# Turning the softmax maxima into a row: a transfer in place of four TensorE transposes

## The chip, the cores and the metric

The kernel runs on one core of a Trainium2 chip. The metric is the device time of one execution in microseconds (us); the median of three runs is compared. Five engines work side by side and are tied by semaphores: TensorE (PE, with its weight loads shown apart as PEld), VectorE (DVE), ScalarE (ACT), GpSimd (POOL) and SyncE, whose queue (SP) issues every transfer of this kernel.

## The reference

Two layers over 1024 latent tokens and 256 context tokens, model width 1024. In each layer one input projection feeds a grouped-query attention (16 query heads and 4 key heads of 64, so four query heads share a key head) and a gated linear recurrence; both are gated, projected, merged and added back. What the change touches is the softmax of the attention:

```python
def gqa(q, k, v):
    s = jnp.einsum('bqkgd,bskd->bkgqs', q, k).astype(jnp.float32)
    p = jax.nn.softmax(s, axis=-1).astype(v.dtype)
    return jnp.einsum('bkgqs,bskd->bqkgd', p, v)
```

A latent query sees 1280 keys, a context query the 256 context keys; the second layer has no context queries.

## The kernel before

The activations lie with features on the partitions, and each layer runs in four stages: queries, keys and values; the recurrence; attention; the output products. The change lies in the attention stage, which runs twice, at about 600 to 1330 us and 2255 to 2905 us of the span.

**Units.** The attention is cut into units of one head and 512 latent queries (64 units: 32 in each layer) or of two heads and 256 context queries (8 units, first layer only). `Unit.load` brings a unit's queries into two tiles of 512 columns, `qa` (high and low halves of the numbers, on 128 partitions) and `qb` (the high halves again on partitions 0 to 63). Partition 64 of `qb` is a row of 512 numbers that the unit fills itself: minus the maximum of each query's scores. Its partner in the keys, row 64 of `k2`, is all ones, so that the product over 65 rows subtracts the maximum while the scores are summed.

**The first pass, for the maxima.** `s1(j, b)` multiplies a block of 128 queries (the stationary operand, a slice of `qa`) with up to 512 keys (the moving operand) into a PSUM tile `s1ps`, queries on the partitions; 0.3 us later in the plan VectorE reduces it to one column of `mp` (line 980). A long unit has twelve such pieces: four blocks by 512, 512 and 256 keys. `smax` reduces `mp` to `mz`, 128 partitions by 4 blocks (line 985). `aug` turns that into the row: four TensorE transposes (line 149) write 1x128 pieces of a PSUM tile `mtps`, and ScalarE copies its 512 numbers, negated, to row 64 of `qb` (line 991).

**The second pass.** `s2(kt)` multiplies 128 keys with all 512 queries in two products, the one with `qa` and the one with `qb` and its row 64; ScalarE takes the exponential twice (`pf` in full precision, `ph` rounded), VectorE the difference `pl` (line 1004), GpSimd adds the `pf` up, and `av(kt)` multiplies both with the values. A long unit has ten of these.

**The order.** TensorE executes in the order in which the program emits; for the other engines and the SP queue the compiler's scheduler may place instructions otherwise. The emission follows a plan: `Timeline` holds a clock that each TensorE instruction advances by a model cost (`mm`, and 0.109 us for each transpose in `tr`), and a heap of events. A unit begins at `g0`, in plan units; long units are 10 apart. Its load stands at `g0` - 14.5, its first-pass pieces from -12.4 to -4.3, `smax` at -3.2, `aug` at -2.0, its `s2(kt)` at `g0` + kt. So units overlap: while one unit runs its second pass, the next runs its first. Between the events TensorE is filled with the input products of the gates (`gps`). `pace` turns plan units into clock time from the sum of all model costs; by the trace a plan unit lasts some 1.95 us in the second layer.

**Tiles.** `ptile("s")` hands out six PSUM banks in turn to `s1ps`, `s2ps`, `mtps`, `lps` and `gps`. `qa` and `qb` have three buffers each.

Of the kernel before, what the change touches and what calls it, by code (L numbers as in the profile page):

```python
# [26 lines left out]
F32 = mybir.dt.float32  # L27
F32R = mybir.dt.float32r
AF = mybir.ActivationFunctionType
OP = mybir.AluOpType  # L30
AX = mybir.AxisListType
# [27 lines left out]
def r32(ap):  # L59
    return ap.bitcast(F32)  # L60
# [40 lines left out]
def trunk_kernel(ctx: ExitStack, tc: tile.TileContext, xT, cc, par, wmod, win, wgate, wo,  # L101
                 rope_c, rope_s, out):
    nc = tc.nc
    V, S, G, DMA = nc.vector, nc.scalar, nc.gpsimd, nc.sync
    ctx.enter_context(tc.manual_schedule(engines={mybir.EngineType.PE}))
    tl = Timeline()
# [8 lines left out]
    def ptile(tag, name):  # L115
        tag = "s" if tag == "g" else tag
        bufs = {"s": 6, "av": 2}[tag]
        return psum.tile([128, 512], F32, name=name, tag=tag, bufs=bufs)
# [16 lines left out]
    def mm(o, a, b, start, stop, cost=None):  # L135
        n = 1
        for d in b.shape[1:]:
            n *= d
        if cost is not None:
            tl.now += cost  # L140
        elif b.dtype == F32R:
            tl.now += 0.216 * n / 512
        else:
            tl.now += max(0.2, 0.858 * n / 512)
        nc.tensor.matmul(o, a, b, start=start, stop=stop)  # L145

    def tr(o, a):
        tl.now += 0.109
        nc.tensor.transpose(o, a, ident)  # L149
# [302 lines left out]
    class Group:  # L452


        def __init__(self, l, tiles, g, chs, store, name):
            self.l, self.tiles, self.g, self.chs, self.store = l, tiles, g, chs, store
            self.qg, self.work = {}, None
            self.parts, self.sq = [chs], {}
            self.o0 = 0 if "C" in chs else CTX
            self.n = TOK - self.o0  # L460
            self.rows = [dtile(l, f"{name}{t}", [2, 2, self.n]) for t in tiles]
# [247 lines left out]
    for l in range(DEPTH):  # L709
# [206 lines left out]
        with tc.tile_pool(name="att", bufs=2, reuse_waits="tile") as work:  # L916
            kv = {}

            def load_kv(g):
                k1 = work.tile([128, TOK], F32R, name="k1", tag="k1")  # L920
                k2 = work.tile([128, TOK], F32R, name="k2", tag="k2")
                t, r0 = g // 2, (g % 2) * 64
                DMA.dma_start(r32(k1[0:64]), dd["k"][t][0, r0:r0 + 64])
                DMA.dma_start(r32(k1[64:128]), dd["k"][t][0, r0:r0 + 64])
                DMA.dma_start(r32(k2[0:64]), dd["k"][t][1, r0:r0 + 64])
                G.memset(r32(k2[64:65]), 1.0)
                v = work.tile([128, 10, 128], F32R, name="vv", tag="vv")
                DMA.dma_start(r32(v), dd["v"][g])
                kv[g] = k1, k2, v
# [4 lines left out]
            def add(g, fn):  # L934
                cnt[0] += 1
                ev.append((g, cnt[0], fn))
# [3 lines left out]
            class Unit:  # L940


                def __init__(self, i, t, c, e, g0):
                    self.i, self.t, self.c, self.e, self.g0 = i, t, c, e, g0
                    self.nkt = 2 if e == 2 else 10
                    self.P = {}
                    late = not last and t and c == "L0" or e == 2
                    add(-24 if i == 0 else g0 - 11.8 if late else g0 - 14.5, self.load)
                    nb = 1 if e == 2 else 3
                    pieces = [(j, b) for j in range(4) for b in range(nb)]  # L950
                    for x, (j, b) in enumerate(pieces):
                        add(g0 - (9.6 - 6.2 * x / len(pieces) if late else 12.4 - 8.8 * x / len(pieces)), lambda j=j, b=b: self.s1(j, b))
                    add(g0 - 3.2, self.smax)
                    add(g0 - 2.0, self.aug)
                    for kt in range(self.nkt):
                        add(g0 + kt, lambda kt=kt: self.s2(kt))
                        add(g0 + kt + 2.8, lambda kt=kt: self.av(kt))
                    add(g0 + self.nkt + 1.85, self.evac)
                    add(g0 + self.nkt + (5.0 if e == 2 else 3.6), self.lsum)
                    self.groups = ((0,), (1,)) if e == 2 else ((0, 1, 2), (3, 4, 5), (6, 7), (8, 9))  # L960
                    self.accs = {}
# [13 lines left out]
                def s1(self, j, b):  # L975
                    k1 = kv[self.t // 2][0]
                    n = 256 if self.e == 2 or b == 2 else 512
                    ps = ptile("s", "s1ps")
                    mm(ps[:, :n], self.qa[:, j * 128:(j + 1) * 128], k1[:, b * 512:b * 512 + n], True, True)
                    tl.at(0.3, lambda: V.reduce_max(self.mp[:, j, b:b + 1], ps[:, :n], axis=AX.X))  # L980

                def smax(self):
                    nb = 1 if self.e == 2 else 3
                    self.mz = work.tile([128, 4], F32, name="mz", tag="mz", bufs=3)
                    V.reduce_max(self.mz, self.mp[:, :, :nb], axis=AX.X)

                def aug(self):
                    pt = ptile("s", "mtps")
                    for j in range(4):
                        tr(pt[0:1, j * 128:(j + 1) * 128], self.mz[:, j:j + 1])  # L990
                    S.activation(self.qb[64:65], pt[0:1, :], AF.Copy, scale=-1.0)

                def s2(self, kt):
                    k1, k2, _ = kv[self.t // 2]
# [103 lines left out]
            g0, cost, i = 5.0, 0.0, 0  # L1098
            for t in range(8):
                if t % 2 == 0:  # L1100
                    add(g0 - 19 if t else -25, lambda t=t: load_kv(t // 2))
                for c, e in [("L0", 0), ("L0", 1), ("L1", 0), ("L1", 1)] + ([] if last else [("C", 2)]):
                    Unit(i, t, c, e, g0)
                    i += 1
                    ctxu = e == 2
                    g0 += 2 if ctxu else 10
                    cost += (4 * 0.108 + 2 * 0.864 + 1.34 if ctxu else 4 * 0.54 + 10 * 0.864 + 1.34)
            ev.sort(key=lambda x: (x[0], x[1]))
            first_g = ev[0][0]
            span = ev[-1][0] - first_g  # L1110
# [226 lines left out]
```

## Time and profile before

| | |
|---|---|
| median of three runs | 3194.48 us (3193.29 to 3196.1) |
| the profiled execution | 3197.96 us, of which the span is 3196.2 us |
| PE busy | 3059.7 us, 96% of the span |
| DVE, ACT, POOL busy | 2457.1, 1749.6, 1020.0 us |
| mean granted TensorE clock | 0.986 |

The span runs from the first to the last instruction of the profiled execution. An engine's busy time is an average over stages with different limits. "Idle before" an instruction is put down to what ended it. The ends of matmuls are modelled, so the distance between two starts says more than a duration.

### The profile page before, as it was taken

To read this page: it belongs to the slowest core of one execution; us is meant where nothing else is said; L and a number is where in the kernel's file an instruction comes from. 1 tells how busy PE (TensorE), PEld (TensorE's weight loads), DVE (VectorE), ACT (ScalarE), POOL (GpSimd) and SP (SyncE) were. 2 spreads that over 40 slices of the span, in tenths; PEclk is the share of its full clock that TensorE was granted. 3 is DMA by queue.
4 is the path that set the end of the run, shared out by engine and by line. 5 is a ranking of instruction groups with operands and counts; after the bars stand their busy time and mean duration, and the time that the engine had idled before them with its cause. 6 is when DMAs were issued, how large, how long until landed. Compare 5 with 4: busy or idle time off the path is not lost. (4 is left out here: it accounts for less than half of the span.)

```text
span 3196.2 us, 42921 instructions
## 1 busy us (share of the span) xinstructions
PE 3059.7 (96%) x14880; PEld 2430.8 (76%) x14880; DVE 2457.1 (77%) x3675; ACT 1749.6 (55%) x3060; POOL 1020.0 (32%) x777
## 2 busy tenths in 40 slices
PE   7999999999999999999899999899999999999999
PEld 3788788777777777787778778777777777777887
DVE  7665887589898988556685785997799999996544
ACT  4323667466666666545555324676477766673222
POOL 0211444234434333234432121433244444441000
PEclk9999999999999999999999999999999999999999
DMA  5443111311222122264555452111412121115554
GB/s 196 144 152 121 50 50 62 115 59 59 73 64 78 60 64 64 87 195 153 172 191 168 147 166 87 60 47 53 121 56 75 58 75 58 52 59 170 181 177 138
DMA packets 233049, 331.95 MB, mean 104 GB/s; under 512 B 53296, under 2 KB 99184, under 8 KB 232576
## 3 DMA queue, kind: packets, MB, share of 16 engines
q1 hardware_dynamic: 232832, 329.21, 32.0%
q8 instruction: 117, 1.92, 0.2%
q14 instruction: 100, 0.82, 0.1%
HBM read 252.54 MB, written 76.58 MB: 103 GB/s over the span
## 5 line engine op out<-in xcount | busy, mean ns | idle before, releaser
L145 PE MATMUL gps<-h,whi 128*128 128x512 f32 x3328 | 1041.4, 394 | 21.1 <-DVE g L876 15.3
L145 PEld LDWEIGHTS gps<-h,whi 128*128 128x128 f32 x3328 | 612.1, 190 | 148.4 <-issue 10.7
L1004 DVE TENSOR_TENSOR pl<-pf,ph 128x512 fp32r<-128x512 f32 x656 | 630.2, 961 | 83.1 <-ACT ph L1003 79.5
L145 PE MATMUL gps<-h,wlo 128*128 128x512 f32 x1664 | 654.5, 393 | 1.3 <-DVE wlo L227 1.3
L1002 ACT ACTIVATE pf<-s2ps 128x512 f32<-128x512 f32 x656 | 392.8, 599 | 348.1 <-issue 157.0
L1018 POOL TENSOR_TENSOR acc<-pf 128x512 f32<-128x512 f32 x256 | 352.0, 1375 | 713.1 <-ACT pf L1002 711.5
L980 DVE TENSOR_REDUCE mp<-s1ps 128x1 f32<-128x512 f32 (+1 forms) x800 | 454.1, 583 | 63.7 <-PE s1ps L145 60.8
L1003 ACT ACTIVATE ph<-s2ps 128x512 fp32r<-128x512 f32 x656 | 390.0, 595 | 0.0
L227 DVE TENSOR_TENSOR wlo<-wraw,whi 128x512 fp32r<-128x512 f32 x392 | 335.3, 878 | 61.4 <-ACT whi L226 32.7
L226 ACT ACTIVATE whi<-wraw 128x512 fp32r<-128x512 f32 x324 | 193.6, 627 | 333.8 <-PE gps L145 258.1
L145 PEld LDWEIGHTS gps<-h,wlo 128*128 128x128 f32 x1664 | 314.3, 189 | 69.9 <-DVE wlo L227 2.0
L145 PE MATMUL s1ps<-k,qa 128*128 128x512 f32 (+1 forms) x800 | 284.9, 363 | 12.3 <-DMA qa<-q0L 10.3
L145 PE MATMUL avps<-ph,vv 128*128 128x512 f32 x656 | 266.9, 407 | 0.0
L145 PE MATMUL avps<-pl,vv 128*128 128x512 f32 x656 | 260.2, 397 | 5.0 <-DVE pl L1004 4.9
L145 PE MATMUL s2ps<-qa,k 128*128 128x512 f32 x656 | 261.1, 398 | 1.8 <-DVE mp L980 1.6
L145 PE MATMUL s2ps<-qb,k 65*128 65x512 f32 x656 | 260.3, 397 | 0.0
L145 PE MATMUL gps<-e,whi 128*128 128x512 f32 x768 | 243.9, 399 | 0.2 <-DVE e L227 0.2
L360 POOL TENSOR_TENSOR macc<-macc,wmt 128x512 f32<-128x512 f32 x112 | 156.2, 1395 | 255.2 <-ACT wmt L358 221.9
L145 PE MATMUL qps<-h,whi 128*128 128x512 f32 x640 | 203.0, 398 | 1.5 <-DVE h L674 0.9
L1020 POOL TENSOR_TENSOR acc<-acc,pf 128x512 f32<-128x512 f32 x128 | 181.5, 1418 | 71.4 <-ACT pf L1002 69.2
L145 PE MATMUL gps<-c,whi 128*128 128x256 f32 x1024 | 197.2, 288 | 3.1 <-DVE c L222 2.1
L145 PEld LDWEIGHTS s1ps<-k,qa 128*128 128x128 f32 x800 | 151.6, 190 | 51.8 <-issue 6.4
(216 smaller groups left out, 5026.6 us busy)
## 6 DMA issues: line engine op xcount, KB each, us to landing
wraw<-in_win_dram SPq DMA_DIRECT2D x200, 256.0 KB
wraw<-in_wo_dram SPq DMA_DIRECT2D x192, 256.0 KB
wm<-in_wmod_dram SPq DMA_DIRECT2D x32, 512.0 KB
wm<-in_wmod_dram SPq DMA_DIRECT2D x8, 1024.0 KB
rb<-rq SPq DMA_DIRECT2D x64, 128.0 KB
k<-k SPq DMA_DIRECT2D x24, 320.0 KB
v<-vst SPq DMA_DIRECT2D x20, 256.0 KB
vv<-v SPq DMA_DIRECT2D x8, 640.0 KB
```

What stands on the lines that cost most here:

```text
L145: nc.tensor.matmul(o, a, b, start=start, stop=stop)
L226: S.activation(dst_hi, src, AF.Copy)
L227: (V if lo_eng == "v" else G).tensor_sub(dst_lo, src, r32(dst_hi))
L360: G.tensor_add(acc, acc, t)
L980: tl.at(0.3, lambda: V.reduce_max(self.mp[:, j, b:b + 1], ps[:, :n], axis=AX.X))
L1002: S.activation(pf, ps, AF.Exp)
L1003: S.activation(ph, ps, AF.Exp)
L1004: tl.at(1.4, lambda: V.tensor_sub(pl, pf, r32(ph)))
L1018: G.tensor_add(self.acc_tile(x), first, pf)
L1020: G.tensor_add(self.accs[x], self.accs[x], pf)
```

## The change

The four transposes, their PSUM tile and ScalarE's copy of 512 numbers in one partition go. ScalarE negates `mz` into a new tile `mr` (128 partitions by 4, three buffers), and a transfer on the SP queue writes `mr` into row 64 of `qb`: partition p gives four neighbouring numbers (16 bytes) at columns 4p to 4p + 3. For the columns to be right, block j of the first pass is no longer queries 128j to 128j + 127 but every fourth query from j on, so the stationary operand of `s1` is read with a step of four numbers. The negation is emitted 0.6 us of plan time after `smax`, the transfer 0.6 us after that; the event `aug` goes, and the cost that sets the pace falls from 1.34 to 0.9 a unit.

```diff
                     add(g0 - 3.2, self.smax)
-                    add(g0 - 2.0, self.aug)
...
-                    mm(ps[:, :n], self.qa[:, j * 128:(j + 1) * 128], k1[:, b * 512:b * 512 + n], True, True)
+                    mm(ps[:, :n], self.qa[:, j:512:4], k1[:, b * 512:b * 512 + n], True, True)
...
                 def smax(self):
+
                     nb = 1 if self.e == 2 else 3
-                    self.mz = work.tile([128, 4], F32, name="mz", tag="mz", bufs=3)
-                    V.reduce_max(self.mz, self.mp[:, :, :nb], axis=AX.X)
-
-                def aug(self):
-                    pt = ptile("s", "mtps")
-                    for j in range(4):
-                        tr(pt[0:1, j * 128:(j + 1) * 128], self.mz[:, j:j + 1])
-                    S.activation(self.qb[64:65], pt[0:1, :], AF.Copy, scale=-1.0)
+                    mz = work.tile([128, 4], F32, name="mz", tag="mz", bufs=3)
+                    mr = work.tile([128, 4], F32R, name="mr", tag="mr", bufs=3)
+                    V.reduce_max(mz, self.mp[:, :, :nb], axis=AX.X)
+
+                    def put():
+                        DMA.dma_start(r32(self.qb[64:65]).rearrange("o (p j) -> o p j", j=4),
+                                      r32(mr))
+
+                    def turn():
+                        S.activation(mr, mz, AF.Copy, scale=-1.0)
+                        tl.at(0.6, put)
+                    tl.at(0.6, turn)
...
-                    cost += (4 * 0.108 + 2 * 0.864 + 1.34 if ctxu else 4 * 0.54 + 10 * 0.864 + 1.34)
+                    cost += (4 * 0.108 + 2 * 0.864 + 0.9 if ctxu else 4 * 0.54 + 10 * 0.864 + 0.9)
```

## Rows read from the trace of the kernel before

**Rows 1.** The page: the span, and busy time of each engine.
```profile
span 3196.2 us, 42921 instructions
PE 3059.7 (96%) x14880; PEld 2430.8 (76%) x14880; DVE 2457.1 (77%) x3675; ACT 1749.6 (55%) x3060; POOL 1020.0 (32%) x777
```
**Rows 2.** Two 80 us windows: PE, PEld, DVE, ACT, POOL busy; clock, DMA share, GB/s.
```profile
1160.00:1240.00 80.00, 78.83 (x387) 60.39 (x386) 71.16 (x119) 53.88 (x101) 30.76 (x24) 1.00 0.20 62
2320.00:2400.00 80.00, 78.85 (x370) 59.13 (x368) 77.76 (x120) 56.74 (x105) 35.99 (x26) 1.00 0.17 54
```
**Rows 3.** Tile mtps: durations in ns min/median/max; then who waited for tile mz.
```profile
L149 PE MATMUL mtps<-ident,mz x288: 268/272/276, 622.6 to 2875.4; 128*1 128x128 f32 x144
L991 ACT ACTIVATE qb<-mtps x72: 584/587/589, 623.3 to 2876.5; 1x512 fp32r<-1x512 f32 x72
...
  PE mtps L149: 5.3, 6
```
**Rows 4.** PE in order of time, second layer: start us, duration, instruction, count.
```profile
2558.40 0.39 PE L145 MATMUL s2ps<-qa,k 128*128 128x512 f32 x1
2558.63 0.39 PE L145 MATMUL s2ps<-qb,k 65*128 65x512 f32 x1
2558.86 0.60 PE L149 MATMUL mtps<-ident,mz 128*1 128x128 f32 x4
2559.21 0.48 PE L145 MATMUL s1ps<-k,qa 128*128 128x512 f32 x1
2559.53 0.39 PE L145 MATMUL avps<-ph,vv 128*128 128x512 f32 x1
...
2562.21 0.40 PE L145 MATMUL s2ps<-qb,k 65*128 65x512 f32 x1
```
**Rows 5.** VectorE in order of time: that unit's maxima.
```profile
2556.59 0.15 DVE L985 TENSOR_REDUCE mz<-mp 128x4 f32<-128x12 f32 x1
```
**Rows 6.** DVE and PE in order of time: the unit with the shortest interval.
```profile
1148.42 0.15 DVE L985 TENSOR_REDUCE mz<-mp 128x4 f32<-128x12 f32 x1
...
1148.63 0.60 PE L149 MATMUL mtps<-ident,mz 128*1 128x128 f32 x4 [0.66 <-DVE mz L985]
...
1152.09 0.40 PE L145 MATMUL s2ps<-qb,k 65*128 65x512 f32 x1
```
**Rows 7.** ScalarE's groups over the span: busy us, mean ns, idle before.
```profile
L1002 ACT ACTIVATE pf<-s2ps 128x512 f32<-128x512 f32 x656 | 392.8, 599 | 348.1 <-issue 157.0 <-PE s2ps L145 148.2 <-POOL acc L1018 22.4
...
L400 ACT ACTIVATE rst<-rst 128x20 f32<-128x20 f32 x12 | 2.6, 219 | 61.1 <-DVE rst L399 38.2 <-issue 22.9
```
**Rows 8.** The SP queue in order of time, same unit.
```profile
2552.05 0.52 SPq L1056 DMA_DIRECT2D ls3L<-lrow  x1
2553.76 0.61 SPq L1071 DMA_DIRECT2D rq<-ls3L  x1
2558.18 0.33 SPq L1080 DMA_DIRECT2D l3L<-rq  x1
2560.42 1.09 SPq L969 DMA_DIRECT2D qa<-q4L  x2
```
**Rows 9.** Transfers from 2558.18 to 2560.18 us, in 40 slices of 0.05 us.
```profile
GB/s 0 0 0 0 0 0 0 0 0 0 0 0 0 0 0 0 10 31 26 14 2 0 0 0 0 0 0 0 0 0 0 0 0 0 0 0 0 0 0 0
```
**Rows 10.** SP queue's waits, 2290 to 2900 us: total us, times, longest.
```profile
SPq L969 <- PE s1ps L145: 104.8, 40, 9.0
```
**Rows 11.** Tile s1ps: its weight loads.
```profile
L145 PEld LDWEIGHTS s1ps<-k,qa x800: 185/189/332, 600.0 to 2870.6; 128*128 128x128 f32 x160
```
**Rows 12.** PE in order of time, first layer: narrow matmuls.
```profile
617.57 0.28 PE L145 MATMUL gps<-c,wlo 128*128 128x256 f32 x1
617.69 0.28 PE L145 MATMUL s1ps<-k,qa 128*128 128x256 f32 x1
```
**Rows 13.** Waits from 2290 to 2900 us: total us, times, longest.
```profile
PEld avps L145 <- DVE pl L1004: 8.5, 10, 2.7
PE lps L145 <- DVE mp L980: 5.2, 4, 2.0
```

## The prediction

> **What bounds the kernel now.** I read the page first, then the busy times by stretch, then TensorE in order of time around one set of transposes, and last the views of what waits for the maxima. The page gives TensorE 96% of the span and VectorE 77% [rows 1]. That is an average; the change acts only in the two attention stages, so the stretches decide. In the first layer TensorE is busy 78.8 of 80 us and VectorE 71.2; in the second TensorE again 78.8, VectorE 77.8, with the granted clock at 1.00 in both [rows 2]. The reader is to see two things there: a microsecond taken from TensorE in these stages is a microsecond of the end, and in the second layer VectorE is 1.1 us of 80 behind it, so it may give part of that back. ScalarE with 54 to 57 us and GpSimd with 31 to 36 have room [rows 2].
>
> **What goes.** There are 288 transposes, four in each of 72 units [rows 3]. Their worth is read from starts, since matmuls overlap. The usual step from one 512-wide matmul to the next is 0.23 us (2558.40 to 2558.63). From the matmul ahead of the transposes at 2558.63 to the second one behind them at 2559.53 it is 0.90, where two steps would be 0.46 [rows 4]. So a set costs 0.90 - 0.46 = 0.44 us, a little more than its own 0.35 because the weight load behind it also comes late. 72 x 0.44 = 31.7 us. TensorE also waited 5.3 us, six times, for the maxima ahead of a set [rows 3]. Together 37.0 us leave TensorE's order.
>
> ScalarE's copy of 512 numbers in one partition, 587 ns [rows 3], becomes a copy of four numbers in 128 partitions. The nearest row is one of 128x20, 219 ns [rows 7]; I take that. The 0.37 us a unit that ScalarE saves is worth nothing, as it has a third of its time free [rows 2]. One PSUM bank fewer is taken in each unit; I count nothing for that. The pace follows the smaller model cost, 0.44 us a unit, which is also what the transposes took: the mix of gate products and units stays.
>
> **What is added: the way of the row.** The row must be in `qb` before the unit's first product over 65 rows. Time for it: the maxima of one unit are reduced at 2556.59 and done at 2556.74 [rows 5]; its first reader starts at 2562.21 [rows 4]. That is 5.5 us. Taken in the same way for all 72 units, the interval is 3.5 us at the shortest (done at 1148.57, read at 1152.09 [rows 6]), 5.5 in the middle, and under 4.7 for 20 units. With the transposes gone it shrinks by 0.44, and for the shortest by its wait of 0.66 too, to 2.4.
>
> Need for it: ScalarE's copy, 0.22, behind at most one pair of exponentials at 0.6 each [rows 7], so 0.2 to 1.4; then the transfer. Its nearest row is the 4 KB one of 128 pieces that goes from 128 partitions to memory: issue begins at 2558.18 [rows 8], and its bytes move in the slices 0.8 to 1.05 us after that [rows 9]. For the completion signal there is a bound: a store issued at 2552.05 has released its follower by 2553.76 [rows 8], 1.7 us at most. So the row needs 1.2 to 3.1 us from the end of the maxima. No row shows 128 pieces of 16 bytes that all land in one partition. Below, nothing can be gained by it. Above, the far end is the load of small pieces issued at 2553.76: its data has been used by 2558.18, when the result of the computation on it is about to issue [rows 8], so 4.4 us at most. With 4.4 the chain would need 4.6 to 5.8 us, about every second unit would wait some 0.7 us, and 25 us would be lost. I take 1.0 to 1.7, because the 128-piece transfer is the same in count and nearly in size; then only the few units that waited for the maxima before wait still. Their wait moves from the transposes to the reader; I give half of it back, 2.5 us.
>
> The Trainium skill, "DMA: Bandwidth & Descriptors", section "Anatomy of one DMA", puts a small transfer at about 2.0 us fixed, most of it completion. The trace's 1.7 bounds it from above for a store to memory. By 2.0 the need would be 3.4 at most and the sum would not move.
>
> **What is moved: the queue.** The transfer joins the SP queue, which issues in order. It takes 0.33 us there [rows 8], 72 times; between the four issues of rows 8 the queue stands idle for 1.2, 3.8 and 1.9 us, so there is room. What comes behind it are the queries of the unit after the next, weights and the sums' transfers, none of them for the unit at hand; I count nothing for their delay of 0.33 us. What stands ahead of it matters more and is the second rival.
>
> **The stepped stationary operand.** The 800 weight loads of the first pass [rows 11] read every fourth number. Each stands under the matmul ahead of it, so it costs only what exceeds the step of 0.23 us. A contiguous load fits into 0.12 us: a narrow first-pass product starts 0.12 after the narrow one ahead of it [rows 12]. No row shows a stepped load. The lower bound is no cost; at twice the time, 0.24, it is just covered behind a 512-wide matmul, and 0.11 shows behind each of the 33 first-pass products that follow a 256-wide one (617.57 to 617.69 is one; the first layer's context products and narrow pieces make all of them). 33 x 0.11 = 3.6 us; if the 0.01 over the step shows too, 767 x 0.01 = 8 us more. I take 3.6.
>
> **VectorE in the second layer.** TensorE already waits for it there: for `pl` 8.5 us, for the first pass's reductions ahead of `lps` 5.2 [rows 13]. 32 units x 0.44 = 14.1 us are to be saved in a stage where VectorE has some 3 to 6% of its time free [rows 2], so savings of 2.3% fit, but its uneven backlog will show more often. I give back a third, 4.7 us.
>
> **The sum.** 37.0 - 2.5 - 3.6 - 4.7 = 26.2 us. The profiled execution took 3197.96 us for a span of 3196.2; it becomes 3171.8. The median of the runs lies 3.5 us below the profiled execution, so I predict 3168 us. All 37 kept gives 3157; 15 kept gives 3179.
>
> **The rivals.**
>
> *VectorE takes most of it back.* For it: 77.8 of 80 us in the second layer [rows 2]. Against it: the first layer, with 40 of the 72 units, has 9 us of 80 free. All of the second layer's 14.1 lost and half of the first layer's 17.6 as well leaves 37.0 - 2.5 - 3.6 - 14.1 - 8.8 = 8 us; without the latter 17. So 3178 to 3186.
>
> *The row stands behind the query loads.* The queue waits at its head: 104.8 us in 40 waits of up to 9 us for TensorE to free a query buffer [rows 10]. In the unit shown the loads got through at 2560.42 [rows 8], 3.7 us after the maxima. If the scheduler put the row behind all three of them, at about 0.54 each, it would issue at 2562.0 and land at 2563.1, when its reader is due at 2562.21 - 0.44 = 2561.8: 1.3 us late in 64 long units, 83 us, so about 3168 + 83 = 3250. It decides from 26 / 72 = 0.36 us of lateness a unit. Against it: the row is ready near 2557.5, 3 us before those loads can go, and the scheduler orders by readiness as it sees it. A mild form, 0.3 to 0.4 us late on average, ends at no change.
>
> *Stepped weight loads take three to four times as long.* At 0.36 or 0.48 us each exceeds the step by 0.13 or 0.25: 800 times, 104 or 200 us, so 3270 to 3365. It decides from 0.23 + 26 / 800 = 0.26 us a load. Against it: nothing in the rows; for it: nothing either. The Trainium skill, "SBUF — State Buffer", section "Door 1: The DMA port swizzle", says that SBUF has lines of 16 bytes, that full bandwidth needs at least two hits a line, and that each crossing costs. With a step of four fp32 numbers every number lies in its own line, so by that rule the loads do slow down; the page gives no factor. By its two hits a line I read a half rate, which is the 3.6 us above; a larger factor is this rival.
>
> **Chances.** Forecast, 3155 to 3180: 0.60. VectorE takes most back: 0.14. Row behind the loads or otherwise late: 0.10 in full, 0.07 mildly (no change). Stepped loads slow: 0.09. A measurement of this kernel tells about 0.2%, 6 us, from no change. Faster: 0.60 + 0.13 = 0.73. Same: 0.01 + 0.07 + 0.01 = 0.09. Slower: 0.18. The range 3154 to 3206 leaves out most of the two slow rivals, 0.17, and little below.
>
> **What would show it.** No `mtps` rows; the matmul behind the last one ahead of them follows at 0.23. The weight loads of `s1ps` at 189 ns [rows 11], or near 0.3 us with steps unchanged if the rate halves; if steps at `s1ps` exceed 0.24, the third rival. The first `s2ps` over 65 rows of a unit shows no idle time put down to a transfer into `qb`; if it does in most units, the second rival, and the SP queue's order tells which form. VectorE's busy share in the second layer rises to 78.5 of 80 and waits for `pl` grow by some 5 us; if they grow by 15, the first rival. The prediction is wrong if any wait appears in every unit, since 0.36 us of it undoes the gain.

## The result and the profile after

The changed kernel takes 3175.74 us (median of four runs, 3169.99 to 3179.46) against 3195.29 for the kernel before on the same chip: a ratio of 0.9936, with a 95% interval of 0.9918 to 0.9954. That is about 20 us faster (15 to 26). The forecast was 26 us and 3168. The profiled execution shown here took 3176.29 us.

The page of the changed kernel, to be held against [rows 1]:

```profile
span 3174.5 us, 42428 instructions
...
PE 3049.5 (96%) x14592; PEld 2459.1 (77%) x14592; DVE 2453.9 (77%) x3675; ACT 1715.0 (54%) x3060; POOL 1024.5 (32%) x777
```

The 288 transposes are gone, and the span is 21.7 us shorter. VectorE does what it did. The two windows of [rows 2] again:

```profile
1160.00:1240.00 80.00, 79.67 (x378) 63.37 (x377) 71.89 (x117) 53.50 (x104) 32.39 (x25) 1.00 0.22 64
2320.00:2400.00 80.00, 78.84 (x357) 61.43 (x356) 78.92 (x120) 55.79 (x107) 36.83 (x26) 1.00 0.19 58
```

In the first layer TensorE is a little fuller than before. In the second VectorE is busy 78.9 of 80 us where 78.5 was foreseen; it has 1.1 us left where it had 2.2, and TensorE still idles.

**The way of the row.** First the view of tile `mr` (durations in ns min/median/max, first and last start), then that of tile `qb`, the line on idle time of an engine until the transfer came (us, times):

```profile
L993 ACT ACTIVATE mr<-mz x72: 194/206/256, 618.0 to 2852.2; 128x4 fp32r<-128x4 f32 x72
L989 SPq DMA_DIRECT2D qb<-mr x72: 501/521/761, 618.2 to 2852.4; - x72
```
```profile
  DMA qb<-mr: 0.5, 1
```

The copy takes 206 ns, where 219 was taken from [rows 7]. The issue takes 0.52 us, not the 0.33 of [rows 8]. One reader of 72 waited for the row, 0.5 us. From the end of the maxima to the last packet it takes 1.68 us in the middle of the 72 and 5.08 at the most; each reader's start is found by counting ten `s2` a long unit, and lies 5.45 us behind the maxima in the middle. One unit of the second layer, the SP queue in order of time:

```profile
2562.38 0.52 SPq L989 DMA_DIRECT2D qb<-mr  x1
2565.31 1.11 SPq L968 DMA_DIRECT2D qa<-q4L  x2
```

Its maxima are done at 2560.99, the row is issued at 2562.38 because ScalarE had a pair of exponentials in hand, and it is read at 2567.10. It goes ahead of the query loads, which are free to go at 2565.31 only.

**The stepped loads.** The view of tile `s1ps`, against [rows 11]:

```profile
L145 PEld LDWEIGHTS s1ps<-k,qa x800: 307/309/334, 598.9 to 2848.8; 128*128 128x128 f32 x160
```

A load takes 309 ns instead of 189. Behind a 512-wide matmul the step stays at 0.23 us. Behind a narrow one it shows. TensorE in order of time, first layer, against [rows 12]:

```profile
616.30 0.28 PE L145 MATMUL gps<-c,wlo 128*128 128x256 f32 x1
616.42 0.39 PE L145 MATMUL s1ps<-k,qa 128*128 128x256 f32 x1
616.65 0.39 PE L145 MATMUL gps<-c,whi 128*128 128x256 f32 x2
```

From 616.42 to 616.65 is 0.23, where a narrow step is 0.12.

**Where the time went, by stage.** The distance between the starts of the first `s1ps` and the last `avps` matmul is the attention stage. The first layer's fell from 730.1 to 715.0 us (600.0 to 1330.1 before, 598.9 to 1313.9 after: 15.1 less), the second's from 645.9 to 640.5 (2254.7 to 2900.6 before, 2237.9 to 2878.5 after: 5.4 less); the other stages are the same within 1.1 us. To see why the second layer gave so little I price each of TensorE's steps at its normal distance (0.2325 us for 512 columns, 0.119 for 256, 0.11 for a transpose) and call the remainder of the stage its rest: waits, late loads and steps at the lower clock. The priced steps fall by 16.9 and 13.4 us. The rest rises from 40.2 to 42.0 in the first layer and from 39.8 to 47.8 in the second. So 8.0 us of the second layer's 13.4 came back as rest.

Weight loads that waited, 2230 to 2900 us (total us, times, longest), against the first of [rows 13] for `pl`:

```profile
PEld avps L145 <- DVE pl L1008: 14.6, 22, 2.3
PEld s1ps L145 <- DVE mp L979: 7.8, 9, 1.7
```

In the kernel before, the same view of weight loads has for `s1ps`, and the view of the matmuls for `gps`:

```profile
PEld s1ps L145 <- DVE mp L980: 1.9, 3, 0.7
```
```profile
PE gps L145 <- DVE mp L980: 3.2, 1, 3.2
```

The waits for `pl` grew from 8.5 us in 10 to 14.6 in 22; some 5 us more were foreseen, it is 6.1. Those of `s1ps` for a reduction grew from 1.9 to 7.8. Others shrank: `lps` waited 5.2 us for reductions [rows 13] and `gps` 3.2, and in the changed kernel the matmuls show

```profile
PE lps L145 <- DVE mp L979: 0.8, 2, 0.6
...
PE gps L145 <- DVE mp L979: 0.2, 1, 0.2
```

So the waits have changed places. Counted by steps (what a step takes over its normal distance, where that is above 0.04 us and the trace puts the wait down to VectorE), VectorE holds TensorE up for 19.7 us of the second layer's stage before and 23.9 after, 4.3 more. The other 3.7 of the 8.0 are spread: 2.0 over some 2,500 steps that are a few ns longer, 0.9 under ScalarE's name, the remainder in smaller items. In the first layer VectorE's part falls from 18.4 to 14.4.

The longest waits look like this on TensorE (the bracket is the wait and its releaser):

```profile
2555.23 0.39 PE L145 MATMUL avps<-ph,vv 128*128 128x512 f32 x1
2557.64 0.50 PE L145 MATMUL avps<-pl,vv 128*128 128x512 f32 x1 [2.02 <-DVE pl L1008]
...
2559.23 0.63 PE L145 MATMUL avps<-ph,vv 128*128 128x512 f32 x1
2559.65 0.63 PE L145 MATMUL avps<-pl,vv 128*128 128x512 f32 x1
```

VectorE in the same stretch:

```profile
2554.14 0.41 DVE L979 TENSOR_REDUCE mp<-s1ps 128x1 f32<-128x256 f32 x1
2554.47 1.44 DVE L1099 TENSOR_TENSOR z<-z,rl 128x512 f32<-128x512 f32 x1
2555.84 1.74 DVE L1008 TENSOR_TENSOR pl<-pf,ph 128x512 fp32r<-128x512 f32 x1
2557.51 0.68 DVE L979 TENSOR_REDUCE mp<-s1ps 128x1 f32<-128x512 f32 x1
```

and GpSimd:

```profile
2553.88 1.49 POOL L1022 TENSOR_TENSOR acc<-pf 128x512 f32<-128x512 f32 x1 [3.21 <-ACT pf L1006]
2555.45 1.59 POOL L1024 TENSOR_TENSOR acc<-acc,pf 128x512 f32<-128x512 f32 x1
```

The end of a pair of units (`done`, lines 1097 and 1099: `rl` by the gates, `z` by `rl`) stands in VectorE's order ahead of a `pl` that TensorE needs. Both `z` and `pl` are stretched while GpSimd adds. TensorE waits 2.0 us, and soon afterwards its granted clock is halved, as two windows show (columns as in [rows 2]):

```profile
2550.00:2557.00 7.00, 5.52 (x27) 3.66 (x26) 7.00 (x11) 3.86 (x7) 3.71 (x3) 1.00 0.05 19
2559.00:2562.50 3.50, 3.50 (x10) 2.75 (x9) 1.99 (x5) 1.96 (x5) 0.65 (x1) 0.51 0.00 0
```

At 0.51, the lower of the two levels, a 512-wide step takes 0.42 us (2559.23 to 2559.65). The second layer's attention spends 13.7 us at that level, before the change as after it, so the clock isn't what took the saving back.

### The profile page after: what moved, and what is told of

It is laid out like the page before. It is cut to its first block, busy times and chain, and to the rows that moved or that the text cites. A ratio compares the mean times of both kernels' runs of the same rounds, so it can differ in the third digit from the quotient of the medians.

```text
span 3174.5 us, 42428 instructions
## 1 busy us (share of the span) xinstructions
PE 3049.5 (96%) x14592; PEld 2459.1 (77%) x14592; DVE 2453.9 (77%) x3675; ACT 1715.0 (54%) x3060; POOL 1024.5 (32%) x777
## 4 chain that ended last, share of the span: by engine, by line
PE 53%; DVE 19%; issue 6%; ACT 4%; DMA 4%; POOL 3%; SPq 0%; DVEq 0%; POOLq 0%; ACTq 0%
PE gps L145 29%; PE avps L145 8%; PE s2ps L145 7%; PE s1ps L145 4%; DVE pl L1008 3%; DVE wlo L227 3%; DVE mp L979 2%; PE lps L145 2%; POOL macc L360 2%; PE gtps L145 1%; DVE ti L856 1%; PE qps L145 1%; POOL b L853 1%; DVE g L867 1%; PE vps L145 1%
## 5 line engine op out<-in xcount | busy, mean ns | idle before, releaser
L145 PEld LDWEIGHTS gps<-h,whi 128*128 128x128 f32 x3328 | 613.5, 190 | 135.3 <-issue 10.7
L145 PE MATMUL s1ps<-k,qa 128*128 128x512 f32 (+1 forms) x800 | 287.3, 368 | 15.9 <-DMA qa<-q0L 10.7
L145 PEld LDWEIGHTS s1ps<-k,qa 128*128 128x128 f32 x800 | 244.5, 310 | 55.4 <-DVE mp L979 10.6
```

## The experiments

All times are medians. The ratio and its interval are to runs of the kernel before on the same chip; its median was 3197.9 us beside runs 1 to 4, 3195.27 beside 5 to 8 on another chip, and 3196.09 beside 9 to 12.

**1. The step alone.** Kernel before, with stepped blocks and transposes that write every fourth column:

```diff
-                    mm(ps[:, :n], self.qa[:, j * 128:(j + 1) * 128], k1[:, b * 512:b * 512 + n], True, True)
+                    mm(ps[:, :n], self.qa[:, j:512:4], k1[:, b * 512:b * 512 + n], True, True)
...
-                        tr(pt[0:1, j * 128:(j + 1) * 128], self.mz[:, j:j + 1])
+                        tr(pt[0:1, j:512:4], self.mz[:, j:j + 1])
```

> The kernel before, with only its blocks of queries taken as every fourth column; the four transposes stay and write every fourth number of their PSUM row. If stepped weight loads are covered by the matmul ahead of them (my theory), the weight loads of s1ps take about 309 ns as in the changed kernel, the step from one 512-wide matmul to the next stays near 0.23 us, and the time is 0 to 5 us above the kernel before. If the loads are where the missing part of the gain went (rival), the time is 6 to 15 us above the kernel before.

Measured: 3209.39 against 3197.9 us, ratio 1.0038 (1.0025 to 1.0051), 12 us slower. TensorE in order of time in this kernel:

```profile
2567.97 0.60 PE L149 MATMUL mtps<-ident,mz 128*1 128x128 f32 x4
2568.33 0.60 PE L145 MATMUL s1ps<-k,qa 128*128 128x512 f32 x1
2568.77 0.39 PE L145 MATMUL avps<-ph,vv 128*128 128x512 f32 x1
```

The `s1` behind the transposes takes 0.44 us to the next step, where [rows 4] have 0.32 (2559.21 to 2559.53). A set of transposes is followed by an `s1` 55 times, and 34 stand behind narrow matmuls: 89 x 0.12 = 10.7 us, which is nearly all of the 12. So the cost of the step hangs on what stands ahead of the load. The theory's 0 to 5 us was a miss: it left out that a slower load isn't covered behind the short transposes either. With the transposes gone, 55 of the 89 places go too.

**2. The change without the step.** Blocks contiguous again, the row by transfer:

```diff
-                    mm(ps[:, :n], self.qa[:, j:512:4], k1[:, b * 512:b * 512 + n], True, True)
+                    mm(ps[:, :n], self.qa[:, j * 128:(j + 1) * 128], k1[:, b * 512:b * 512 + n], True, True)
```

> The changed kernel with contiguous blocks of queries: weight loads back at 189 ns, the row still brought by the transfer. It leaves out the right order of the maxima in the row, and scales the queries by 0.0005 instead of 0.125 so that the exponentials stay finite. If the steps are covered, 0 to 4 us faster than the changed kernel's 3176. If the steps cost the missing part, 8 to 15 us faster, 3161 to 3168.

Measured: 3178.25 us, 0.9941 (0.9929 to 0.9954). The whole time can't tell it from the changed kernel. The rows can: 29 first-pass products stand behind narrow ones in both kernels, and the steps from them to the next matmul take 10.5 us in all with the step and 8.1 without it, so the step costs 2.3 us.

**3. No way of the row at all.** As 2, with neither `mr` nor the transfer; GpSimd sets the row to zero.

```diff
+                    G.memset(r32(qb[64:65]), 0.0)
...
-                    tl.at(0.6, turn)
```

> As the last one, but without ScalarE's negation and without the transfer: GpSimd sets the row to zero when the queries are loaded. It leaves out the subtraction of the maxima. It bounds what the row's way costs: ScalarE waits 23.6 us in all for the maxima in the changed kernel, and the queue is held too. If that way is hidden (my theory), within 3 us of the last kernel. If ScalarE's wait delays the exponentials and so TensorE (rival), 5 to 12 us faster than the last kernel, most of it in the second layer.

Measured: 3175.42 us, 0.9931 (0.9917 to 0.9944), the changed kernel's time. Against run 2 that is 2.8 us less, within the noise of some 6. The negation, the transfer and their wait cost nothing that can be told, and the second layer's shortfall stays without them: its stage takes 643.3 us.

**4. The old pace.** The changed kernel with the old model cost.

```diff
-                    cost += (4 * 0.108 + 2 * 0.864 + 0.9 if ctxu else 4 * 0.54 + 10 * 0.864 + 0.9)
+                    cost += (4 * 0.108 + 2 * 0.864 + 1.34 if ctxu else 4 * 0.54 + 10 * 0.864 + 1.34)
```

> The changed kernel with the cost that sets the pace back at 1.34 a unit. If the second layer's missing gain comes from VectorE's limit, the pace hardly matters: within 4 us of the changed kernel. If it comes from the new order of units against gate products (rival), the time moves by more than 5 us.

Measured: 3177.4 us, 0.9937 (0.9924 to 0.9951): the whole time does not move. The stages do. At the old pace 1401 and 915 `gps` matmuls lie in the two attention stages, where the changed kernel has 1314 and 855 (the kernel before 1308 and 852), so these stages take 736.3 and 647.3 us and what follows each of them is shorter. The rest in the second is 40.7 us, hardly more than the 39.8 of the kernel before, where the changed kernel has 47.8; some 3 us of that difference are less time at the lower clock (6.8 us instead of 13.7). From the first `s1ps` of the second layer to the end run 4 takes 928.6 us and the changed kernel 936.5; from the first layer's to the second's it takes 1648.5 against 1639.0. So, as far as one profiled execution of each can tell, the second layer keeps most of its saving at the old pace and the first loses about as much more.

**5 and 6. Less work for VectorE.** The narrow pieces of the first pass are not reduced, in the kernel before (5) and in the changed one (6), 105 us less for VectorE:

```diff
-                    tl.at(0.3, lambda: V.reduce_max(self.mp[:, j, b:b + 1], ps[:, :n], axis=AX.X))
+                    if b < 2:
+                        tl.at(0.3, lambda: V.reduce_max(self.mp[:, j, b:b + 1], ps[:, :n], axis=AX.X))
```

> The kernel before with less work on VectorE: the narrow first-pass pieces (keys 1024 to 1279 of long units) are still multiplied but not reduced, 256 reductions of about 0.41 us, 105 us of VectorE in all. The maxima are over 1024 of the 1280 keys, and the queries are scaled by 0.0005. It is the partner of the next kernel. If VectorE limits the second layer, it is 10 to 20 us faster than the kernel before, most of it in the second layer.

> The changed kernel with the same reductions left out. If the part of the gain that is missing in the second layer went to VectorE (my theory), the change is worth 27 to 35 us between these two kernels, and the second layer's attention shortens by 10 to 14 us between them, where it was 5 with the full work. If the missing part is an accident of the new order (rival), the difference stays near 20 and the second layer's near 5.

Measured: 3178.14 us (0.9945, 0.9931 to 0.9958) and 3160.52 us (0.9893, 0.9880 to 0.9907). Each kernel gains 15 to 17 us, and the change is worth 17.6 us between them (12 to 24), no more than with all the work. My theory's 27 to 35 was a miss: VectorE's total work is not what took the saving back. A second miss: most of run 5's gain was expected in the second layer, and it came in the first (730.1 to 714.3 us, against 645.9 to 641.6).

**7. The maxima later.** `smax` at `g0` - 1.8 in the plan instead of - 3.2.

```diff
-                    add(g0 - 3.2, self.smax)
+                    add(g0 - 1.8, self.smax)
```

> The changed kernel with the reduction to the maxima 1.4 plan units (about 2.7 us) later, at g0 - 1.8. The trace of the changed kernel shows 5.4 us in the middle between the maxima and the row's first reader, of which the row's way takes about 1.7 to its last packet. If that interval is what hides the transfer (my theory), it shrinks to about 2.7; some 10 to 30 units wait for the row, 3 to 20 us in all, and the time is 3178 to 3195. If the row were later than I think (rival), the wait shows in nearly every unit and the gain is gone, over 3200.

Measured: 3182.16 us, 0.9952 (0.9939 to 0.9964), 6 us above the changed kernel, which the two intervals do not tell from none. Now the row is waited for, as its waits from 597 to 2900 us show (total us, times, longest):

```profile
PEld s2ps L145 <- DMA qb<-mr: 14.3, 9, 2.5
PE s2ps L145 <- DMA qb<-mr: 11.6, 9, 2.1
```

Nine readers of 72 run out of slack. The edit moved less than was meant: from the maxima to the reader it is now 5.22 us in the middle of the 72 and 2.22 at the least, where the changed kernel has 5.45 and 2.69, and 2.7 in the middle was expected. So VectorE reduces most units' maxima about when it did before. The shortest case tells what the way needs when nothing stands ahead of it: the last packet is there 1.63 us after the maxima and the waiting reader starts at 2.22. The way of the row is hidden by its early start, not by being short; how much of the slack could go is not measured.

**8. Narrow pieces merged, in the changed kernel.** The 256-wide products of two blocks go side by side into one PSUM tile, and one reduction makes both maxima:

```diff
+                    if b == 2 and j % 2 == 0:
+                        return
...
+                        if b == 1 and j % 2:
+                            self.nar = ptile("s", "s1ps")
+                            mm(self.nar[:, 0:256], lhs(j - 1), k1[:, 1024:1280], True, True)
+                    else:
+                        nar = self.nar
+                        mm(nar[:, 256:512], lhs(j), k1[:, 1024:1280], True, True)
+                        tl.at(0.3, lambda: V.reduce_max(self.mp[:, j - 1:j + 1, 2],
+                                                        nar.rearrange("p (x n) -> p x n", x=2), axis=AX.X))
```

> The changed kernel with the narrow first-pass pieces of two blocks side by side in one PSUM tile and reduced by one instruction: 128 reductions of about 0.69 us in place of 256 of 0.41, 17 us less of VectorE, the same products on TensorE. If VectorE limits the second layer, 3 to 8 us faster than the changed kernel. If not, or if the PSUM bank held longer costs as much, within 3 us or slower.

Measured: 3155.61 us, 0.9872 (0.9856 to 0.9888), 20 us faster than the changed kernel and much more than was expected. The second layer's attention takes 625.0 us. Its waits for `mp` at the first pass have nearly gone (weight loads, 2230 to 2900 us):

```profile
PEld avps L145 <- DVE pl L1020: 11.5, 20, 1.4
...
PEld s1ps L145 <- DVE mp L983: 1.4, 4, 0.5
```

**9 to 11. The `done` pair on GpSimd.** From the stretch shown above I formed a new theory, that bursts in VectorE's order (the pair ahead of a `pl`) took the saving back. The pair is moved in the kernel before (9), in the changed one (10), and in the changed one with merged pieces (11):

```diff
-                    S.activation(row[0:32 * ng], lp[0:32 * ng], AF.Copy)
+                    S.activation(row[0:32 * ng], lp[0:32 * ng], AF.Copy, scale=2.0)
...
-                    V.scalar_tensor_tensor(rl[:, :n], rl[:, :n], 0.5, gates[self.t][:, off:off + n],
-                                           op0=OP.mult, op1=OP.mult)
-                    V.tensor_mul(z, z, rl[:, :n])
+                    G.tensor_mul(rl[:, :n], rl[:, :n], gates[self.t][:, off:off + n])
+                    G.tensor_mul(z, z, rl[:, :n])
```

> The kernel before, with the two products at the end of a unit pair (rl by gates, z by rl) on GpSimd instead of VectorE; the factor 0.5 is folded into ScalarE's copy of the sums, so the output is the same. This takes 26 us of VectorE's work out of the second layer, in bursts of some 1.8 us, and puts it on GpSimd, which was busy a third of the time. Theory (bursts in VectorE's order make TensorE wait for pl): the second layer's attention gets shorter by 1 to 4 us, the whole by 2 to 6 (3189 to 3193 us), little because the transposes still give VectorE a head start of 0.44 us a unit. Rival (the waits in the second layer come from VectorE's reductions alone, the pair only happens to stand beside them): no change within 2 us. Second rival (GpSimd and VectorE slow each other): 2 us or more slower.

> The changed kernel with the same move of the pair of products to GpSimd. Theory of bursts: the waits for pl in the second layer (13.6 us) fall by half, the stage of 640.9 us gets 5 to 8 us shorter, the whole 3166 to 3170 us, so the change is worth more (22 to 26 us) between this kernel and the one before with the same move than between the two kernels themselves (20). Rival (reductions alone): within 2 us of the changed kernel's 3176. Second rival (GpSimd and VectorE slow each other): 3178 or more.

> The changed kernel with both: the narrow pieces of two blocks side by side in one PSUM tile with one reduction (as in the run of that name, 3155.6 us), and the pair of products on GpSimd. Theory of bursts: another 2 to 5 us off, 3151 to 3154 us, less than without the merging because the merged reductions leave fewer waits. Rival (reductions alone): 3154 to 3158. Second rival (GpSimd and VectorE slow each other): 3158 or more.

Measured: 3177.23 us (0.9940, 0.9925 to 0.9955), 3157.41 us (0.9873, 0.9856 to 0.9890) and 3151.47 us (0.9859, 0.9845 to 0.9872). Weight loads waiting for `pl`, 2230 to 2900 us, in run 9 and then in run 10:

```profile
PEld avps L145 <- DVE pl L1004: 2.6, 6, 0.7
```
```profile
PEld avps L145 <- DVE pl L1008: 6.4, 11, 1.3
```

Runs 9 and 10 are misses. The pair costs much more than expected, 19 us of the time in the kernel before and 18 in the changed one, and the theory's ranges, 3189 to 3193 and 3166 to 3170, lie well above both. It is 62 us of VectorE's time in the kernel before, where the 105 us of reductions that run 5 leaves out cost 17, so the amount alone does not set the price; whether it is the pair's place in VectorE's order or the way GpSimd stretches it is not told apart. It costs the same with and without the transposes: the change is worth 19.8 us between runs 9 and 10 (13 to 27). The pair isn't what took the saving back. Run 11 is the fastest version found, 1.41% under the kernel before and inside the 3151 to 3154 that were expected. Its two gains, 20 and 18 us by themselves, make 24 together, as if they removed the same waits.

**12. Narrow pieces merged, in the kernel before.** The edit of run 8, with the contiguous blocks and the transposes:

```diff
+                    lhs = lambda x: self.qa[:, x * 128:(x + 1) * 128]
...
+                            self.nar = ptile("s", "s1ps")
+                            mm(self.nar[:, 0:256], lhs(j - 1), k1[:, 1024:1280], True, True)
```

> The kernel before (contiguous blocks, transposes) with the narrow pieces of two blocks side by side in one PSUM tile and one reduction for both. Theory: merging pays most where TensorE is tight against VectorE, so before the change it gains 5 to 12 us (3183 to 3190 us), and the change is worth 28 to 34 us between this kernel and the merged changed one (3155.6). Rival (merging pays by itself, fewer reductions and fewer PSUM tiles, whatever the transposes do): 3173 to 3178 us, and the change is worth 18 to 22 us in either company.

Measured: 3184.58 us, 0.9964 (0.9952 to 0.9976), as the theory had it. Merging gains 11.5 us before the change and 20 after it, so between runs 12 and 8 the change is worth 29.0 us; from the two intervals, taken as independent and on two chips, 23 to 36. That is 9 us more than between the two kernels as they are, some 1 to 18.

**The four pairs side by side** (stage times and rest as above, from one profiled execution each; the worth from medians, in us):

| | first layer | second layer | rest, first | rest, second | worth |
|---|---|---|---|---|---|
| as they are | 730.1 to 715.0 | 645.9 to 640.5 | 40.2 to 42.0 | 39.8 to 47.8 | 19.6 |
| narrow pieces not reduced (5, 6) | 714.3 to 703.6 | 641.6 to 637.9 | 24.4 to 30.6 | 35.5 to 45.1 | 17.6 |
| `done` pair on GpSimd (9, 10) | 719.7 to 707.9 | 629.8 to 626.0 | 29.8 to 34.9 | 23.6 to 33.2 | 19.8 |
| narrow pieces merged (12, 8) | 732.5 to 708.7 | 637.1 to 625.0 | 42.6 to 35.7 | 31.0 to 32.3 | 29.0 |

Runs of one kernel spread over 3 to 14 us, and the profile of run 9 is the fastest of its six, so single stage times are good to some 5 us. In three pairs the rest of the second layer rises by 8 to 10 us, in the merged pair by 1. The merged pair differs as much in the first layer: there the rest falls by 7 us in the merged pair and rises by 2 to 6 in the others. A part of that has a name. In run 12 the transposes wait longer for the maxima than the 5.3 us in 6 waits of [rows 3], and the change takes these waits out together with the transposes; from 597 to 1330 us and from 2230 to 2900:

```profile
PE mtps L149 <- DVE mz L997: 7.1, 8, 1.3
```
```profile
PE mtps L149 <- DVE mz L997: 2.2, 3, 0.9
```

The stage times of the merged pair fall by 35.9 us in all, its profiled spans by 26.9 only: between the two attention stages run 8 took 929.0 us with 67 of them at the lower clock, run 12 took 921.4 with 51.

## Why the prediction was right, and where it was off

The sign, the place and most of the size held: 3175.7 lies in the forecast's own range of 3155 to 3180, near its upper end; 6.6 of the 26.2 us that were summed up did not come.

- *The transposes, 31.7 us.* The priced steps fall by 16.9 + 13.4 = 30.3 us, which is 31.7 less nine more gate products in the stages; the price of 0.11 is the prediction's own, so this only says that the transposes are gone. The price holds over all 72 sets of the kernel before: from a transpose to the next start it is 0.089 us in the mean, and the matmul behind a set takes 0.084 more than normal, 4 x 0.089 + 0.084 = 0.44. Right. The mix of gate products and units stayed, as was said.
- *The waits for the maxima, 5.3 us gone and 2.5 back.* They are gone, and one wait of 0.5 us for the row stands in their place. Counted by steps the waits for the maxima held TensorE up for 6.8 us, all in the first layer, and there VectorE's part as a whole fell by 4.0: so 2.8 came back elsewhere in the order, near the 2.5 that was set. The first layer's rest rose by 1.8 us all the same, with the stepped loads, longer waits for ScalarE and many steps of a few ns.
- *The stepped loads, 3.6 us.* 2.3 by the rows of runs with and without the step, 0.11 at a narrow product, as priced. The rate was guessed well: 120 ns more a load, 1.6 times where twice was taken. The Trainium skill, "SBUF — State Buffer", section "Door 1: The DMA port swizzle", asks for two hits in a line of 16 bytes; the slower load agrees with it, and the third rival's factor of three or four does not appear.
- *VectorE in the second layer, 4.7 us.* This is the term that fell short: 8.0 came back in that layer. VectorE's name stands on 4.3 of it in the changed kernel's trace, but on 8.1 of 9.1 and 10.2 of 10.8 in runs 2 and 3, whose stage is as long; so between half and nearly all of it is waiting for VectorE. My sum left 14.1 - 4.7 = 9.4 us for that layer and it kept 5.4; for the first it left 16.8 and that kept 15.1. The 4 us here are most of the 5.7 by which the sum, 26.2, stands above the two stages' 20.5. The reason given, an uneven backlog, isn't refuted, but the figure that I drew the size from, VectorE's free time, doesn't set it: taking 105 us of work away, half of it in this layer, leaves the rise at 9.6 us.
- *The row behind the query loads.* Its order was as argued: the row goes 2.9 us ahead of them in the unit shown. Run 3 shows that it costs nothing that can be told, run 7 that a reader waits where the slack is gone, 11.6 us in nine waits of TensorE. The section of the Trainium skill that the prediction names for a small transfer, "Anatomy of one DMA" in "DMA: Bandwidth & Descriptors", has its 2.0 us for transfers that GpSimd issues; for this one on the SP queue run 7's shortest case has 1.96 us from issue to reader.
- *VectorE takes most of it back* is right for the second layer alone, which lost 8 of 13.4 us, not all of it to VectorE by name.

What takes the 8 us back is shown only so far: it is neither the step (2), the row (3), VectorE's total work (5, 6), the `done` pair (9, 10) nor the clock. At the old pace (4) it is nearly gone from the second layer, where each unit then has as much TensorE time as before the change, and the first layer loses about as much more. That points to VectorE's work of a unit against the length of a unit, but it is one execution and not shown. The loss also goes where the narrow pieces are merged. Merging changes three things at once: 64 reductions of 0.68 us in the layer instead of 128 of 0.41, ten PSUM tiles a long unit instead of twelve, and another place of the narrow products in TensorE's order. Runs 5 and 6 speak against the reductions' time by itself. Which of the other two it is, was not tried and stays open.

## What to carry to other kernels

Work taken from the bounding engine can come back in part as waits for the engine just behind it, and here that part did not follow from the latter's busy share: it stayed when 105 us of its work were left out. Add up all waits by name, those that shrank too, and look at what stands ahead of the late result. Compare a time by stage as well as in whole, as run 4 shows. Try a second change together with the first one, in all four combinations: merging alone looked like 11.5 us, the change alone like 20, and both are worth 40. A transfer in place of on-engine work is free where the reader has slack; take some of the slack away, and check in the trace that it went.

## What the runs showed of the hardware

- **VectorE is held up by GpSimd, by the kind of operands.** In the changed kernel's second layer, `pl` (two operands in SBUF) takes 0.68 us when no GpSimd instruction overlaps it (128 times) and 1.18 in the mean, 1.81 at the most, when one does (192 times). The 512-wide reductions from PSUM take 0.68 either way (140 and 116 times). The Trainium skill, "SBUF — State Buffer", section "SBUF: two separate sides", says that a VectorE instruction with two SBUF inputs and a GpSimd instruction that reads SBUF exclude each other for a whole instruction. The rows agree: the `pl` of 2555.84 ends at 2557.58, 0.54 us after the add of 2555.45 has ended. So do the others: of 161 `pl` that start while a GpSimd instruction is running 157 end 0.5 to 0.7 us after its end, and the 31 that start ahead of one take 0.67 to 0.68. The products of the `done` pair, of the same form, take 1.1 us in the mean.
- **A stepped stationary operand costs by what stands ahead of it:** 12 us in a kernel with short transposes (run 1), 2.3 without (by the steps of the changed kernel and of run 2), at the same 309 ns a load.
- **A wait can cost more than its length:** after the wait of 2.0 us the granted clock stood at 0.51 from 2559.0 to 2562.5, and steps took 0.42 us instead of 0.23. Not each such wait is followed by this: in the kernel before one of 2.27 us at 2693.7 was not.
- **A small transfer to one partition:** the row's 128 pieces of 16 bytes have all moved 1.37 us after its issue begins (median of 72), and a reader that waits for it starts some 0.6 us after that (run 7).
